# A transformer trunk's FFN: sixteen of twenty-two feature tiles of the second product by Strassen's scheme

## The chip, the cores and the metric

The kernel runs on one core of a Trainium2 chip. A core has TensorE (PE) for matrix products, which reads SBUF and writes PSUM; VectorE (DVE), ScalarE (ACT) and GpSimd (POOL) for elementwise work; and SyncE (SP), which here issues the DMAs. The metric is the device time of one execution in microseconds. Before the change the median of three runs is 2638.42 us (2637.98 to 2640.49).

## The reference, cut to what matters

Four layers work on x of 512 tokens by 1024 columns, in float32. Each has a token mixer (latent attention, retention, gated linear attention, and latent attention again) and then a dense FFN:

```
def swiglu_ffn(x, w_in, w_out):            # w_in 1024 x 5632, w_out 2816 x 1024
    gate, up = jnp.split(x @ w_in, 2, axis=-1)
    return (jax.nn.silu(gate) * up) @ w_out
x = layer_norm(DEEPNORM_ALPHA * x + mixer(x), ln_g[i, 0], ln_b[i, 0])
x = layer_norm(DEEPNORM_ALPHA * x + swiglu_ffn(x, ffn_w_in[i], ffn_w_out[i]), ln_g[i, 1], ln_b[i, 1])
```

## The kernel before

Every product is made of three matmuls (`mm3`, L126). Each float32 operand is split into a high part, a cast by ScalarE to the type that TensorE multiplies, and a low part, the rest, by a subtraction on VectorE (`split`, L101). The terms are high x high, high x low and low x high.

Weights come in chunks of 512 KB (`wcols`, `wload`): a DMA on SP's queue into one of three raw buffers `wraw`, and then `wsplit` (L116) into one of six pairs `whi`, `wlo`. For the first six chunks after a layer norm that ends a sub-layer (`relieve`), GpSimd makes the low part instead of VectorE, so that VectorE is free for the norm.

The FFN (`ffn`, L298) has 22 feature tiles of 128. For each tile the first product takes two weight chunks (gate and up), each 8 x 3 matmuls with the weights stationary and all 512 tokens moving. `evac` then takes silu(gate) on ScalarE and the product with up on VectorE, and splits the result h into a pair of tiles. The first three tiles go in two halves of 256 tokens, since the last tokens of x are not yet transposed.

The second product (`out_proj`, L213) follows when all 22 tiles are there: h is stationary by token tiles of 128, w_out moves by halves of 512 columns. For half 0, four PSUM tiles, one for each token tile, gather all 22 features, and `acc` (L178) adds them to alpha x x. For half 1, `out_tail` (L240) does the same until the last eight features; it keeps their four weight chunks and finishes one token tile after the other, 24 matmuls each, with the layer norm (`ln_finish`, L188) behind each. The transposes for the next mixer (`flush`, L165) are set two token tiles later. For few features (`nf <= 4`) `out_proj` instead loads all weight chunks first and goes by token tiles with both halves. Only mixers took that path.

PSUM has eight banks: six tiles of tag `ps` and two of tag `tp` for transposes. SBUF working tiles come from one pool in each phase (`phase`, L78), by tags with a number of buffers.

The order of instructions on each engine is fixed before the run: a scheduler takes the instructions in the order of the program as their priority, with times that it assumes for each, and hands out buffers as they come free by those times. At run time each engine follows its list in order and waits on semaphores.

Of the kernel before, what the change touches and what calls it, by code (L numbers as in the profile page):

```python
# [9 lines left out]
F32 = mybir.dt.float32  # L10
F32R = mybir.dt.float32r
I32 = mybir.dt.int32
AF = mybir.ActivationFunctionType
ALU = mybir.AluOpType
AX = mybir.AxisListType

P = 128
# [5 lines left out]
ALPHA = (2.0 * DEPTH) ** 0.25  # L23
# [3 lines left out]
NF = F // P  # L27
# [23 lines left out]
class Trunk:  # L51
# [25 lines left out]
    @contextmanager  # L77
    def phase(self, **tags):  # L78

        with self.tc.tile_pool(name="phase", bufs=1, reuse_waits="tile") as self.bp:  # L80
            self.tags = dict(tags, b=self.nb - sum(tags.values()))
            yield

    def b(self, shape=(P, 512), dt=F32, name="b", tag="b"):
# [127 lines left out]

    def out_proj(self, st, w, nf, coef, last, out=None, halves=(0, 1)):  # L213
        wf = lambda f0, half: self.wcols(w, f0 * P, 2, half * 512, 512)
        if nf <= 4:
            ch = {(c, hf): wf(2 * c, hf) for hf in halves for c in range(nf // 2)}
            for t in range(NT):
                for hf in halves:
                    ps = self.ps()
                    for f in range(nf):  # L220
                        if last and hf == 0 and f == 3:
                            self.flush(t - 2)
                        w2 = ch[f // 2, hf]
                        self.mm3(ps, st(f, t), (w2[0][:, f % 2, :], w2[1][:, f % 2, :]), f == 0, f == nf - 1)
                    self.acc(t, hf, ps, coef, last)
                if last:
                    self.ln_finish(t, out)
            self.relieve = 6 if last else 0
            return
        pss = [self.ps() for _ in range(NT)]  # L230
        for f in range(nf):
            if f % 2 == 0:
                w2 = wf(f, 0)
            for t in range(NT):
                self.mm3(pss[t], st(f, t), (w2[0][:, f % 2, :], w2[1][:, f % 2, :]), f == 0, f == nf - 1)
        for t in range(NT):
            self.acc(t, 0, pss[t], coef, last)
        self.out_tail(st, lambda f0: wf(f0, 1), nf, coef, last, out)
# [56 lines left out]
            self.proj_tile(t, wk, n, evac)  # L295


    def ffn(self, l, out=None):  # L298
        nc = self.nc
        w_in, w_out = self.ins["ffn_w_in"][l], self.ins["ffn_w_out"][l]  # L300
        hs = []

        def evac(pg, pu):
            s = self.b()
            nc.scalar.activation(s, pg, AF.Silu)
            nc.vector.tensor_tensor(s, pu, s, op=ALU.mult)  # L306
            h = self.bpair()
            self.split(h[0], h[1], s)
            hs.append(h)

        nh = 3
        first = []
        for f in range(nh):
            wg = self.wcols(w_in, 0, KT, f * P, P)
            wu = self.wcols(w_in, 0, KT, F + f * P, P)
            first.append((wg, self.ps()))
            first.append((wu, self.ps()))
        for t0 in (0, 2):
            for n, (w2, ps) in enumerate(first):
                self.proj_f(w2, ps[:, t0 * P : (t0 + 2) * P], KT, lambda k: self.xm(k, t0, t0 + 2))  # L320
                if n % 2:
                    self.flush(2 + n // 2)
        for f in range(nh):
            evac(first[2 * f][1], first[2 * f + 1][1])
        rot = False
        for f in range(nh, NF):
            if f == nh + 1:
                rot = self.before(l + 1, nc.vector)
            if f == NF - 4 and rot:
                self.rope_sin()  # L330
            wg = self.wcols(w_in, 0, KT, f * P, P)
            pg = self.ps()
            self.proj_f(wg, pg, KT, self.xm)
            wu = self.wcols(w_in, 0, KT, F + f * P, P)
            pu = self.ps()
            self.proj_f(wu, pu, KT, self.xm)
            evac(pg, pu)
        self.ln_begin(l, 1)
        st = lambda f, t: (hs[f][0][:, t * P : (t + 1) * P], hs[f][1][:, t * P : (t + 1) * P])
        self.out_proj(st, w_out, NF, ALPHA, True, out)  # L340

    def load_x(self, x):

# [805 lines left out]
    def run(self, out):  # L1149
        self.load_x(self.ins["x"][0])  # L1150
        for i in range(DEPTH):
            self.mixer(i)
            with self.phase():
                self.ffn(i, out[0] if i == DEPTH - 1 else None)


# [38 lines left out]
```

## Time and profile before

| what | value |
|---|---|
| median of three runs | 2638.42 us |
| the profiled execution | 2635.14 us |
| its span, first to last instruction | 2633.3 us |
| mean granted TensorE clock | 0.994 |
| TensorE busy | 2578.4 us (98%) |
| VectorE busy | 1416.0 us (54%) |
| ScalarE busy | 905.5 us (34%) |
| GpSimd busy | 220.6 us (8%) |
| DMA, mean over the span | 88 GB/s |

The rows further down come from one profiled execution. "L103" is a line of the kernel. A row of the timeline has the start, the duration, the engine, the line, the operation and its tiles (out<-in), and in brackets the idle time of that engine just before it with what ended it. The four FFNs lie at about 250 to 607, 1056 to 1410, 1675 to 2028 and 2270 to 2622 us.

### The profile page before, as it was taken

What the parts mean: (1) busy time and instruction counts of PE and PEld (TensorE: products, weight loads), DVE (VectorE), ACT (ScalarE), POOL (GpSimd) and SP (SyncE); (2) the same over time, 40 slices, a digit from 0 to 9 for tenths busy, and PEclk for the clock granted to TensorE, in tenths of its full rate; (3) what the DMA queues carried; (4) which work ended last, traced back from release to release, by engine and by line L of the source; (5) the groups of instructions that cost most, each with busy time, mean ns of one, the idle gap of its engine ahead of it and who ended that gap; (6) DMA issues with size and microseconds to landing.
All of it is one profiled execution on the core that took longest, in us unless ns stands there. A gap on an engine that the chain in (4) does not pass through costs nothing.

```text
span 2633.3 us, 32309 instructions
## 1 busy us (share of the span) xinstructions
PE 2578.4 (98%) x12996; PEld 2191.5 (83%) x12996; DVE 1416.0 (54%) x2484; ACT 905.5 (34%) x1381; POOL 220.6 (8%) x231
## 2 busy tenths in 40 slices
PE   7999999999999999999999999999999999999998
PEld 6888888887888888988888998888888788888886
DVE  6877433228755548333326888833335686633334
ACT  4652323213333332322213654322312564322221
POOL 3002000001110103000002011100002200100001
PEclk9999999999999999999999999999999999999999
DMA  4212433233223232333233212333322221333321
GB/s 144 73 41 68 128 96 96 96 96 88 77 76 95 89 92 83 103 98 97 96 95 95 76 61 65 109 96 96 96 96 77 70 74 46 100 96 97 99 93 56
DMA packets 294711, 232.35 MB, mean 88 GB/s; under 512 B 21120, under 2 KB 244480, under 8 KB 294560
## 3 DMA queue, kind: packets, MB, share of 16 engines
q1 hardware_dynamic: 294560, 230.28, 28.8%
q8 instruction: 102, 1.67, 0.3%
q14 instruction: 49, 0.40, 0.0%
HBM read 228.15 MB, written 2.10 MB: 87 GB/s over the span
## 4 chain that ended last, share of the span: by engine, by line
PE 85%; DVE 9%; POOL 2%; issue 2%; ACT 2%; DMA 1%; DVEq 0%; SPq 0%; ACTq 0%; POOLq 0%
PE ps L128 27%; PE ps L130 27%; PE ps L129 27%; DVE xt L205 2%; DVE xt L206 1%; PE tp L557 1%; DVE lnst L186 1%; DVE xl L103 1%; PE ps L538 1%; DVE lnu L145 1%; PE ps L537 1%; DMA wraw<-in_mla_w_down 0%; DVE xt L184 0%; PE tp L158 0%; DVE bl L103 0%
## 5 line engine op out<-in xcount | busy, mean ns | idle before, releaser
L102 ACT CAST whi<-wraw 128x1024 fp32r<-128x1024 f32 (+3 forms) x414 | 431.0, 1042 | 1122.3 <-PE ps L130 379.4
L103 DVE TENSOR_TENSOR wlo<-wraw,whi 128x1024 fp32r<-128x1024 f32 (+2 forms) x366 | 444.1, 1215 | 660.4 <-ACT whi L102 647.8
L129 PE MATMUL ps<-xl,whi 128*128 128x512 f32 (+1 forms) x1792 | 659.9, 368 | 7.9 <-DVE xl L103 7.9
L128 PE MATMUL ps<-xh,whi 128*128 128x512 f32 (+1 forms) x1792 | 660.3, 368 | 0.0
L130 PE MATMUL ps<-xh,wlo 128*128 128x512 f32 (+1 forms) x1792 | 659.4, 368 | 0.0
L129 PEld LDWEIGHTS ps<-xl,whi 128*128 128x128 f32 x1792 | 341.2, 190 | 63.1 <-DVE xl L103 8.7
L128 PEld LDWEIGHTS ps<-xh,whi 128*128 128x128 f32 x1792 | 341.2, 190 | 54.9 <-issue 0.4
L130 PEld LDWEIGHTS ps<-xh,wlo 128*128 128x128 f32 x1792 | 341.0, 190 | 55.1
L128 PE MATMUL ps<-whi,bh 128*128 128x512 f32 (+1 forms) x960 | 368.7, 384 | 0.2 <-ACT bh L102 0.2
L130 PE MATMUL ps<-whi,bl 128*128 128x512 f32 (+1 forms) x960 | 367.2, 383 | 0.0
L129 PE MATMUL ps<-wlo,bh 128*128 128x512 f32 (+1 forms) x960 | 367.0, 382 | 0.0
L130 PE MATMUL ps<-whi,xl 128*128 128x512 f32 (+3 forms) x752 | 262.9, 350 | 5.2 <-DVE xl L103 5.2
L128 PE MATMUL ps<-whi,xh 128*128 128x512 f32 (+3 forms) x752 | 264.9, 352 | 1.1 <-ACT xh L102 1.1
L129 PE MATMUL ps<-wlo,xh 128*128 128x512 f32 (+3 forms) x752 | 262.1, 349 | 0.1
L103 POOL TENSOR_TENSOR wlo<-wraw,whi 128x1024 fp32r<-128x1024 f32 (+4 forms) x48 | 118.8, 2490 | 1649.1 <-ACT whi L102 1637.0
L130 PEld LDWEIGHTS ps<-whi,bl 128*128 128x128 f32 x960 | 180.5, 188 | 35.5 <-DVE bl L103 0.5
L128 PEld LDWEIGHTS ps<-whi,bh 128*128 128x128 f32 x960 | 180.5, 188 | 35.0 <-ACT bh L102 0.8
L129 PEld LDWEIGHTS ps<-wlo,bh 128*128 128x128 f32 x960 | 180.5, 188 | 34.7
L306 DVE TENSOR_TENSOR b<-ps,b 128x512 f32<-128x512 f32 x88 | 60.8, 691 | 262.1 <-PE ps L130 261.4
L130 PEld LDWEIGHTS ps<-whi,xl 128*128 128x128 f32 x752 | 142.8, 190 | 23.3 <-DVE xl L103 6.4
L128 PEld LDWEIGHTS ps<-whi,xh 128*128 128x128 f32 x752 | 143.2, 190 | 18.7 <-ACT xh L102 1.5
L129 PEld LDWEIGHTS ps<-wlo,xh 128*128 128x128 f32 x752 | 143.0, 190 | 17.3 <-POOL wlo L103 0.5
(220 smaller groups left out, 2772.6 us busy)
## 6 DMA issues: line engine op xcount, KB each, us to landing
wraw<-in_ffn_w_in SPq DMA_DIRECT2D x176, 512.0 KB, 3.8
wraw<-in_ffn_w_out SPq DMA_DIRECT2D x88, 512.0 KB, 3.3
wraw<-in_ret_w_in SPq DMA_DIRECT2D x48, 512.0 KB, 3.8
wraw<-in_gla_w_in SPq DMA_DIRECT2D x22, 512.0 KB, 3.5
wraw<-in_mla_w_o SPq DMA_DIRECT2D x16, 512.0 KB, 3.9
wraw<-in_ret_w_o SPq DMA_DIRECT2D x16, 512.0 KB, 4.7
wraw<-in_mla_w_down SPq DMA_DIRECT2D x8, 512.0 KB, 4.4
wraw<-in_mla_w_ukv SPq DMA_DIRECT2D x8, 512.0 KB, 3.7
```

The source lines that it names most:

```text
L102: a = self.nc.scalar.copy(hi, src)
L103: b = (eng or self.nc.vector).tensor_tensor(lo, src, hi.bitcast(F32), op=ALU.subtract)
L128: mm(out, s[0], m[0], start=start, stop=False)
L129: mm(out, s[0], m[1], start=False, stop=False)
L130: mm(out, s[1], m[0], start=False, stop=stop)
L145: stt(u, y, y, x, op0=ALU.mult, op1=ALU.mult)
L186: nc.vector.bn_stats(self.stats[t][:, half * 6 : half * 6 + 6], x)
L205: nc.vector.scalar_tensor_tensor(x[:, sl], x[:, sl], mv[:, 0:1], self.g[:, sl], op0=ALU.subtract, op1=ALU.mult)
L206: nc.vector.scalar_tensor_tensor(x[:, sl], x[:, sl], r, self.bb[:, sl], op0=ALU.mult, op1=ALU.add)
L306: nc.vector.tensor_tensor(s, pu, s, op=ALU.mult)
L537: nc.tensor.matmul(ps, qr[:, sl], krh, start=False, stop=False)
L538: nc.tensor.matmul(ps, qr[:, sl], krz[e], start=False, stop=True)
```

## The change

For the first 16 feature tiles the second product becomes a 2 x 2 block product. The blocks of h are (tokens 0 to 255, 256 to 511) x (even, odd feature tile of a pair), those of w_out (even, odd tile) x (columns 0 to 511, 512 to 1023). Seven products of blocks, in Winograd's form, take the place of eight.

- `evac` writes the four h blocks of a pair of tiles into one tile `ft`, and GpSimd makes three sums and differences more (four instructions, with one in place). The seven factors of 128 x 256 are split together (`fh`, `fl`, 1792 elements for each partition).
- `ffn_out` (new) handles a chunk of two pairs, that is four feature tiles. It loads the four weight blocks, makes their sums in place on VectorE (four subtractions), splits each factor (seven splits instead of four), multiplies (for each product two token tiles x two pairs x three matmuls), and adds each result to one or two blocks of x in SBUF, or to a shared sum `u` that is added to three blocks at the end.
- A chunk starts after the first product of the tile behind its last one (tiles 4, 8, 12, 16). Its seven products are dealt out two, two, two and one behind the next four tiles; the last chunk's over the last six.
- The last six tiles go the plain way, now by the path by token tiles (`nf <= 6`): six weight chunks are loaded first, and each token tile takes 36 matmuls.
- The FFN's phase has its own numbers of buffers: 8 of `fh`, 1 of `ft`, 3 of `t` for weight blocks, 1 of `u`, 10 of `b`.

```diff
--- before.py
+++ after.py
@@ -78,7 +78,7 @@
     def phase(self, **tags):
 
         with self.tc.tile_pool(name="phase", bufs=1, reuse_waits="tile") as self.bp:
-            self.tags = dict(tags, b=self.nb - sum(tags.values()))
+            self.tags = {"b": self.nb - sum(tags.values()), **tags}
             yield
 
     def b(self, shape=(P, 512), dt=F32, name="b", tag="b"):
@@ -212,7 +212,7 @@
 
     def out_proj(self, st, w, nf, coef, last, out=None, halves=(0, 1)):
         wf = lambda f0, half: self.wcols(w, f0 * P, 2, half * 512, 512)
-        if nf <= 4:
+        if nf <= 6:
             ch = {(c, hf): wf(2 * c, hf) for hf in halves for c in range(nf // 2)}
             for t in range(NT):
                 for hf in halves:
@@ -295,18 +295,44 @@
             self.proj_tile(t, wk, n, evac)
 
 
     def ffn(self, l, out=None):
         nc = self.nc
         w_in, w_out = self.ins["ffn_w_in"][l], self.ins["ffn_w_out"][l]
-        hs = []
-        def evac(pg, pu):
+        ns = 16
+        self.fact, hs = {}, {}
+        self.u = self.b((P, 2, 512), tag="u", name="u")
+        half = lambda a: a.rearrange("p (a n) -> p a n", a=2)
+        def evac(f, pg, pu):
             s = self.b()
             nc.scalar.activation(s, pg, AF.Silu)
-            nc.vector.tensor_tensor(s, pu, s, op=ALU.mult)
-            h = self.bpair()
-            self.split(h[0], h[1], s)
-            hs.append(h)
+            if f >= ns:
+                if f < NF - 2:
+                    if f % 2 == 0:
+                        self.hp = self.b((P, 2, 512), F32R, "hh", "fh"), self.b((P, 2, 512), F32R, "hl", "fh")
+                    h = tuple(x[:, f % 2, :] for x in self.hp)
+                else:
+                    h = self.bpair()
+                nc.vector.tensor_tensor(s, pu, s, op=ALU.mult)
+                self.split(h[0], h[1], s)
+                hs[f] = h
+                return
+            if f % 2 == 0:
+                self.ft = self.b((P, 7, 256), tag="ft", name="ft")
+            ft = self.ft
+            nc.vector.tensor_tensor(ft[:, 2:4, :] if f % 2 else ft[:, 1::-1, :], half(pu), half(s), op=ALU.mult)
+            if f % 2:
+                tt = nc.gpsimd.tensor_tensor
+                tt(ft[:, 4, :], ft[:, 0, :], ft[:, 3, :], op=ALU.add)
+                tt(ft[:, 5, :], ft[:, 4, :], ft[:, 1, :], op=ALU.subtract)
+                tt(ft[:, 0, :], ft[:, 1, :], ft[:, 0, :], op=ALU.subtract)
+                tt(ft[:, 6, :], ft[:, 2, :], ft[:, 5, :], op=ALU.subtract)
+                h = self.b((P, 7, 256), F32R, "fh", "fh"), self.b((P, 7, 256), F32R, "fl", "fh")
+                self.split(h[0], h[1], ft)
+                self.fact[f // 2] = h
 
         nh = 3
         first = []
@@ -321,8 +347,9 @@
                 if n % 2:
                     self.flush(2 + n // 2)
         for f in range(nh):
-            evac(first[2 * f][1], first[2 * f + 1][1])
+            evac(f, first[2 * f][1], first[2 * f + 1][1])
         rot = False
+        todo = []
         for f in range(nh, NF):
             if f == nh + 1:
                 rot = self.before(l + 1, nc.vector)
@@ -334,10 +361,84 @@
             wu = self.wcols(w_in, 0, KT, F + f * P, P)
             pu = self.ps()
             self.proj_f(wu, pu, KT, self.xm)
-            evac(pg, pu)
+            evac(f, pg, pu)
+            if 4 <= f < ns + 4 and f % 4 == 0:
+                c = f // 4 - 1
+                todo = self.ffn_out(w_out, 2 * c, 2, c == 0)
+            left = (4 - f % 4) if f < ns else NF - f
+            for _ in range(-(-len(todo) // left) if todo else 0):
+                todo.pop(0)()
+        for tt in range(2):
+            for hf, c in ((0, 1), (1, 0), (1, 1)):
+                x = self.xt[2 * hf + tt][:, c * 512 : c * 512 + 512]
+                nc.vector.tensor_tensor(x, x, self.u[:, tt, :], op=ALU.add)
         self.ln_begin(l, 1)
-        st = lambda f, t: (hs[f][0][:, t * P : (t + 1) * P], hs[f][1][:, t * P : (t + 1) * P])
-        self.out_proj(st, w_out, NF, ALPHA, True, out)
+        st = lambda f, t: tuple(x[:, t * P : (t + 1) * P] for x in hs[ns + f])
+        self.out_proj(st, w_out[ns * P :], NF - ns, None, True, out)
+    def ffn_out(self, w, g0, n, begin):
+        nc = self.nc
+        rows = w[2 * g0 * P : 2 * (g0 + n) * P, :].rearrange("(g a p) c -> a p g c", a=2, p=P)
+        B = {}
+        def load(name, a, c, t):
+            nc.sync.dma_start(t, rows[a][:, :, c * 512 : c * 512 + 512])
+            B[name] = t
+        wt = lambda: self.b((P, n, 512), name="wt", tag="t")
+        sub = lambda to, x, y: nc.vector.tensor_tensor(B[to], B[x], B[y], op=ALU.subtract)
+        def product(name, slot, to, u=None):
+            hi, lo = self.wsplit(B[name], n, 512)
+            ps = [self.ps() for _ in range(2)]
+            for tt in range(2):
+                for i in range(n):
+                    s2 = tuple(x[:, slot, tt * P : (tt + 1) * P] for x in self.fact[g0 + i])
+                    self.mm3(ps[tt], s2, (hi[:, i, :], lo[:, i, :]), i == 0, i == n - 1)
+                for hf, c, first in to:
+                    self.acc(2 * hf + tt, c, ps[tt], ALPHA if first else None, False)
+                if u is not None:
+                    x = self.u[:, tt, :]
+                    if u:
+                        nc.scalar.copy(x, ps[tt])
+                    else:
+                        nc.vector.tensor_tensor(x, ps[tt], x, op=ALU.add)
+        s3, a11, a12, a22, s1, s2, s4 = range(7)
+        def p1():
+            load("1", 0, 0, self.wp.tile([P, n, 512], F32, tag="wraw", name="wraw", bufs=self.nraw))
+            load("2", 0, 1, wt())
+            load("3", 1, 1, wt())
+            product("1", a11, [(0, 0, begin)], begin)
+        def p5():
+            sub("1", "2", "1")
+            product("1", s1, [(0, 1, begin), (1, 1, begin)])
+        def p6():
+            sub("1", "3", "1")
+            load("4", 1, 0, wt())
+            product("1", s2, [], False)
+        def p2():
+            product("4", a12, [(0, 0, False)])
+        def p3():
+            sub("4", "4", "1")
+            sub("2", "3", "2")
+            product("3", s4, [(0, 1, False)])
+        def p7():
+            product("2", s3, [(1, 0, begin), (1, 1, False)])
+        def p4():
+            product("4", a22, [(1, 0, False)])
+        return [p1, p5, p6, p2, p3, p7, p4]
 
     def load_x(self, x):
 
@@ -1150,7 +1251,7 @@
         self.load_x(self.ins["x"][0])
         for i in range(DEPTH):
             self.mixer(i)
-            with self.phase():
+            with self.phase(fh=8, ft=1, t=3, u=1, b=10):
                 self.ffn(i, out[0] if i == DEPTH - 1 else None)
```

## Rows read from the trace of the kernel before

**Rows 1.** The page's busy times, with share of the span and instructions of each engine

```profile
PE 2578.4 (98%) x12996; PEld 2191.5 (83%) x12996; DVE 1416.0 (54%) x2484; ACT 905.5 (34%) x1381; POOL 220.6 (8%) x231
```

**Rows 2.** Busy us of each engine in stretches, with granted clock, DMA share and GB/s

```profile
262.00:592.00 330.00, 330.00 (x1524) 276.30 (x1524) 116.20 (x135) 90.52 (x109) 4.79 (x2) 1.00 0.34 102
...
2280.00:2617.00 337.00, 337.00 (x1552) 281.87 (x1551) 116.03 (x140) 88.10 (x106) 2.60 (x2) 1.00 0.30 91
```

**Rows 3.** Timeline of TensorE, first product: start us, us, instruction

```profile
359.69 0.39 PE L129 MATMUL ps<-xl,whi 128*128 128x512 f32 x1
...
371.93 0.39 PE L129 MATMUL ps<-xl,whi 128*128 128x512 f32 x1
```

**Rows 4.** Timeline of ScalarE and VectorE there; in brackets idle time before, and releaser

```profile
360.84 1.05 ACT L102 CAST whi<-wraw 128x1024 fp32r<-128x1024 f32 x1 [3.84 <-PE ps L129]
...
361.93 1.23 DVE L103 TENSOR_TENSOR wlo<-wraw,whi 128x1024 fp32r<-128x1024 f32 x1 [3.62 <-ACT whi L102]
...
366.54 0.69 DVE L306 TENSOR_TENSOR b<-ps,b 128x512 f32<-128x512 f32 x1 [3.38 <-PE ps L130]
```

**Rows 5.** Groups by form: line, engine, operation, shapes, count, busy us, mean ns of one

```profile
L103 DVE TENSOR_TENSOR wlo<-wraw,whi 128x1024 fp32r<-128x1024 f32 x355 | 435.6, 1228 | 652.5 <-ACT whi L102 640.1
...
L102 ACT CAST whi<-wraw 128x1024 fp32r<-128x1024 f32 x397 | 418.3, 1054 | 1104.4 <-issue 371.8 <-PE ps L130 370.1 <-PE ps L129 314.2
...
L103 POOL TENSOR_TENSOR wlo<-wraw,whi 128x1024 fp32r<-128x1024 f32 x42 | 106.4, 2549 | 1272.1 <-ACT whi L102 1260.1 <-DVE xt L184 9.0 <-issue 3.0
...
L103 DVE TENSOR_TENSOR bl<-b,bh 128x512 fp32r<-128x512 f32 x148 | 101.3, 685 | 12.3 <-ACT bh L102 12.0
...
L102 ACT CAST bh<-b 128x512 fp32r<-128x512 f32 x148 | 91.8, 621 | 57.6 <-DVE b L679 20.8 <-DVE b L753 19.0 <-DVE b L1024 11.1
...
L184 DVE SCALAR_TENSOR_TENSOR xt<-xt,ps 128x512 f32<-128x512 f32 x64 | 43.0, 682 | 77.3 <-PE ps L130 77.2
...
L792 POOL TENSOR_TENSOR b<-b 128x512 f32<-128x512 f32 x16 | 22.0, 1377 | 338.8 <-DVE gny L149 246.5 <-DVE b L791 82.7 <-DVE gny L147 8.1
```

**Rows 6.** DMA issues: buffer<-tensor, queue, operation, count, KB each, median us to landing

```profile
wraw<-in_ffn_w_in SPq DMA_DIRECT2D x176, 512.0 KB, 3.8
wraw<-in_ffn_w_out SPq DMA_DIRECT2D x88, 512.0 KB, 3.3
```

**Rows 7.** Timeline of GpSimd at the first FFN's end

```profile
579.81 2.40 POOL L103 TENSOR_TENSOR wlo<-wraw,whi 128x1024 fp32r<-128x1024 f32 x1 [334.43 <-ACT whi L102]
...
585.25 2.40 POOL L103 TENSOR_TENSOR wlo<-wraw,whi 128x1024 fp32r<-128x1024 f32 x1 [3.04 <-ACT whi L102]
...
603.82 10.22 POOL L103 TENSOR_TENSOR wlo<-wraw,whi 128x1024 fp32r<-128x1024 f32 x4 [16.17 <-ACT whi L102]
```

**Rows 8.** Timeline of VectorE at the first FFN's end

```profile
603.51 0.74 DVE L205 SCALAR_TENSOR_TENSOR xt<-xt,lnmv,ln_g 128x512 f32<-128x512 f32 x1
...
604.24 2.84 DVE L205 SCALAR_TENSOR_TENSOR xt<-xt,lnmv,ln_g 128x512 f32<-128x512 f32 x1
...
609.27 0.68 DVE L103 TENSOR_TENSOR xl<-tp,xh 128x512 fp32r<-128x512 f32 x1
```

**Rows 9.** Timeline of TensorE at the start of the second mixer

```profile
623.57 0.80 PE L130 MATMUL ps<-whi,xl 128*128 128x512 f32 x1 [3.75 <-DVE xl L103]
...
625.01 0.63 PE L130 MATMUL ps<-whi,xl 128*128 128x512 f32 x1
625.44 0.63 PE L128 MATMUL ps<-whi,xh 128*128 128x512 f32 x1
```

**Rows 10.** Timeline of TensorE and VectorE at the kernel's end

```profile
2622.17 0.39 PE L130 MATMUL ps<-whi,bl 128*128 128x512 f32 x1
...
2622.60 0.69 DVE L184 SCALAR_TENSOR_TENSOR xt<-xt,ps 128x512 f32<-128x512 f32 x1
...
2624.42 0.96 DVE L205 SCALAR_TENSOR_TENSOR xt<-xt,lnmv,ln_g 128x512 f32<-128x512 f32 x1
...
2625.37 1.68 DVE L205 SCALAR_TENSOR_TENSOR xt<-xt,lnmv,ln_g 128x512 f32<-128x512 f32 x1
```

## The prediction

> **What bounds the kernel now.** I read the page's busy shares first: TensorE works 98% of the span, VectorE 54%, ScalarE 34%, GpSimd 8% [rows 1]. Busy shares mix stages, so next the stretches. In the FFN of a layer TensorE is busy in every microsecond, at granted clock 1.00 (the 2.4 GHz level); VectorE is busy about 35% of it, ScalarE 27%, GpSimd under 2%. The first and the last layer stand there; the two between read alike [rows 2]. So in the FFN the time is the number of matmuls by their pitch. The pitch comes from the starts, not from the 0.39 us of one record, since records overlap: 54 starts lie between 359.69 and 371.93 us, that is 0.2267 us each [rows 3]. What would have to break for another engine to count is the lead of the weights: ScalarE's cast of a weight chunk waits for TensorE to give back one of six hi/lo pairs, and VectorE then stands idle over 3 us, twice for each feature tile [rows 4].
>
> **Matmuls.** The second product of 16 feature tiles takes 16 tiles x 4 token tiles x 2 column halves x 3 terms = 384 matmuls of 512 columns. By the scheme it is 4 chunks x 7 products x 2 token tiles x 2 pairs x 3 terms = 336. So 48 go in each layer, 192 in all, and the other six tiles keep their 144. The new ones have the same form (128x128 stationary, 512 moving), so the same pitch: 192 x 0.2267 = 43.5 us. Since TensorE has no idle time there, all of it comes off the span, unless something new makes it wait.
>
> A sentence on a rule against this: the Trainium skill (TensorE: Matmul & The Clock Gate, "Back-to-back issue gap") gives 131 ns as the sustained spacing of 512-column matmuls in a real kernel. By that, the removed ones would give only 192 x 0.131 = 25 us. The trace disagrees: 0.2267 us over 54 in a row.
>
> **VectorE.** Durations by shape are in [rows 5]. For one chunk of four tiles: 7 weight splits instead of 4, at 1.23 us; 4 weight subtractions of the same shape at 1.23 (bounds 1.23 and, if it ran as two pieces of 512, 2 x 0.69); 16 additions of a product into x at 0.68; 4 into the shared sum u at 0.68. That is 8.6 + 4.9 + 10.9 + 2.7 = 27.1 us against 4.9 before. The factor tile has 1792 elements where two h tiles had 512 each: from 0.685 us at 512 and 1.228 at 1024 its low part comes to 2.04 us against 1.37. Over a layer: 4 x 22.2 + 8 x 0.67 + 6 last additions of u x 0.69, less 1.4 us of u that goes to ScalarE, is 97 us. In the densest four tiles of the first product TensorE has 4 x 48 + 84 = 276 matmuls, 62.6 us. VectorE has 8 x 1.23 + 4 multiplies x 0.69 [rows 4] + 2 x 2.04 + 27.1 = 43.8 us: 70%, not a bound. In layers 0 and 2 the rotary tables of the next layer fall into the first chunk and press it more.
>
> **ScalarE** gets 3 more casts a chunk at 1.05 us and 8 longer casts a layer (1.70 us by the same line through 621 and 1054 ns, against 1.24), with two copies 18 us a layer beside 90. It stays far from a bound.
>
> **GpSimd** makes the four factor sums of a pair, of 128x256. No row has that shape: 0.64 us (a quarter of 2.55 for 128x1024) and 1.38 us (what 128x512 takes) bound it; I take 0.79, on the line through these two rows. That is 25 us a layer.
>
> **DMA.** Each chunk loads four 512 KB pieces, as four tiles did. But three of them now go to tiles of their own, and the first keeps one of three raw buffers from the first product to the fifth, so first-product loads run two deep instead of three, for two loads in 11 to 16 us. Loads land in under 4 us [rows 6]; the six hi/lo pairs, used at 15 per 62.6 us, still give about 25 us of lead. The SP queue gets chunk loads between the others; a load that waits for its tile holds up those behind it, which the lead covers. I cost this at nothing; without the lead a landing of 4 us would show in full.
>
> **New waits, by the nearest margin.** A chunk's first product needs the factors of the tile pair just made. After the pair's last matmul: multiply 0.69, four GpSimd sums 3.2 (2.6 to 5.5), cast 1.70, low part 2.04, together 7.6 us (7.0 to 9.9). The cover is the next tile's 48 matmuls, 10.9 us, and the first five matmuls of the product, 1.1: 12.0 us, and 2.7 more in all but a layer's first chunk, whose predecessor's last product lies between. Spare: 4.4 us, or 7.1. Queueing eats from it: VectorE takes its instructions in order and is 70% taken. Behind a late factor step there stand weight splits (25 us of lead) and additions that free PSUM buffers (six, of which two products and one tile use six; a buffer is wanted again after some 10 us). I take 1 us a layer, 4 us (0 to 20).
>
> **The port that GpSimd and VectorE share.** At the end of the first FFN, four weight splits on GpSimd run back to back, 10.22 us for four where one alone takes 2.40 [rows 7]. Meanwhile VectorE's instructions with two SBUF operands wait for the ends of these: one takes 2.84 us, where the same form just before took 0.74; one with PSUM as a source passes at 0.68 [rows 8]. So VectorE loses, GpSimd hardly does: 0.16 us an instruction. For the factor sums: at most 8 x 0.79 = 6 us a chunk on VectorE, which brings it to 80%.
>
> **The hand-over to the next mixer.** Before, two of six hi/lo pairs were free, so the next mixer's first two splits ran 22 to 28 us before the FFN's end at 607.4, and four at it [rows 7]. After, the tail's six chunks hold all six pairs until the last token tile, so six splits of 2.55 us crowd about its end, and each lets about one two-operand instruction of VectorE's layer norm through. Against that, a token tile of the tail lasts 36 matmuls, 8.2 us, instead of 24, 5.4, so each norm starts 2.7 us sooner before the end. At the first hand-over TensorE already waits 3.75 us for VectorE, and its next matmuls run slow, 0.43 us apart [rows 9]. Two more splits are 5.1 us of blocked VectorE, less 2.7: +2.4 there; the two other hand-overs show smaller waits, I take +1 each: +4 in all (-8 to +15).
>
> **The end.** The last matmul starts at 2622.17 and the last token tile's addition at 2622.60, right behind it; but in the norm that follows, an instruction of 0.74 us takes 1.68, beside GpSimd's part of the norm before [rows 10]. With 8.2 us for each token tile GpSimd is done with that part sooner, and that one and its neighbour (0.96) are back at 0.74: -1.2 us.
>
> **Sum.** The profiled execution took 2635.14 us, span 2633.3 and 1.8 around it; the median of three runs is 2638.42, 3.3 more. -43.5 + 4 + 4 - 1.2 = -36.7, so 2598.4 profiled and 2601.7 as a median.
>
> **Rivals.**
> *Half the gain goes to small waits.* Products wait for subtracted weights, buffers or factors, 1 to 2 us for each of 16 chunks, since the engines' order is written down ahead of the run and VectorE is full at places. For it: 80% with the port; against it: 25 us of lead. At 1.3 us a chunk, 21 us in place of the 4: 2619.
> *Slower: the factor chain lies bare.* If each GpSimd sum waits out a VectorE split (4 x 1.23 = 4.9), both VectorE steps wait 2 us behind others and the cast 1.05, the 7.6 us become 17.6; TensorE then waits 5.6 us at a layer's first chunk and 2.9 at three more, 14.3 a layer, 57 in all in place of the 4: 2601.7 - 4 + 57 = 2655. It decides from 2.7 us a chunk (43.5 / 16). Against it: in the rows it is VectorE that waits. The Trainium skill (SBUF — State Buffer, "Who interferes with whom") says that whichever starts first holds the shared ports for the whole instruction; by that rule GpSimd can lose as VectorE does, and the 4.9 us would be real. The trace shows the one side only.
> *The hand-overs cost 8 us each*, with weights late and the clock down after each wait: 24 us instead of 4: 2622.
> *The rule of 131 ns.* If a removed matmul frees less than its pitch, because others close up already, 25 us come off: 2638.4 - 25 + 6.8 = 2620. Against it is the even pitch.
>
> **Chances.** Forecast 0.63, its own range 2590 to 2615 (the lower end: hand-overs better by 8, no waits among the products); half the gain 0.17; bare chain 0.12; hand-overs 0.06; the rule 0.02. The range 2590 to 2632 leaves out the bare chain and the worst of the half gains, and little below. Within 0.2% (5.3 us, about what measurement can tell from no change) I put 0.05, of the worst half gains and the mildest bare chains; slower 0.11; faster 0.84.
>
> **What would show it.** Right: 192 fewer matmuls at the same pitch; FFN stretches still without TensorE idle time, each some 10 us shorter; VectorE near 1800 us busy, GpSimd near 320; the first wait after the FFN near 6 us. Wrong: TensorE idle at the first product of chunks, released by the factor tile's low part or its cast (bare chain) or by a weight's low part (half gain); over 10 us of waits behind each FFN (hand-over). The forecast fails if idle time within the FFNs passes 20 us.

## The result, and the profile after

The changed kernel takes 2599.7 us (median of four runs, 2595.45 to 2601.17) against 2638.2 for the kernel before (also of four): a ratio of 0.9852, with a 95% interval of 0.9835 to 0.9869. Forecast were 2601.7 us and a range of 2590 to 2632. The profiled execution took 2595.45 us, its span 2593.7; that is 39.6 us under the span of before.

The page's busy times after, which answer to [rows 1]:

```profile
PE 2536.9 (98%) x12804; PEld 2156.5 (83%) x12804; DVE 1792.7 (69%) x2900; ACT 974.6 (38%) x1405; POOL 335.7 (13%) x359
```

There are 192 matmuls fewer, 12804 for 12996. VectorE has 377 us more and GpSimd 115 us. Two stretches of the FFNs after, to be held against [rows 2] (TensorE's busy time comes first behind the length, then weight loads, VectorE, ScalarE, GpSimd, granted clock, DMA share, GB/s):

```profile
262.00:592.00 330.00, 330.00 (x1533) 276.35 (x1532) 220.54 (x269) 109.69 (x119) 30.96 (x33) 1.00 0.31 94
...
2270.00:2580.00 310.00, 310.00 (x1369) 256.69 (x1368) 202.79 (x245) 98.21 (x106) 31.32 (x32) 1.00 0.29 89
```

TensorE still has no idle time there, and the two FFNs between read the same. VectorE went from 35% to 67%. The pitch of the new matmuls, from the first and the last of 24 in two products, to be held against [rows 3]:

```profile
300.81 0.39 PE L128 MATMUL ps<-whi,fh 128*128 128x512 f32 x1
...
306.02 0.39 PE L130 MATMUL ps<-whi,fl 128*128 128x512 f32 x1
```

From the first start to the last there are 23 pitches in 5.21 us, 0.2265 us each (0.2267 before). From its first silu to its last matmul the second FFN takes 330.45 us for 341.33 before; the difference of 10.88 us is 48 x 0.2267. The other three give 10.86 to 10.88.

Where the 39.6 us came from, by stages of the two traces:

| stage | forecast | measured |
|---|---|---|
| matmuls of the four FFNs | -43.5 | -43.5 |
| waits inside the FFNs | +4 | 0 |
| three hand-overs to a mixer | +4 | +6.1 |
| the end, from the last matmul | -1.2 | -2.1 |
| the start, to the first silu | 0 | -0.2 |
| span | -36.7 | -39.6 |

The hand-overs are read from the stretches between the last matmul of one FFN and the first silu of the next. They hold a whole mixer each, which the change does not touch, and the first matmuls of the next FFN. Before:

```profile
607.20:1068.30 461.10, 453.65 (x2115) 378.85 (x2114) 292.91 (x559) 148.65 (x189) 67.32 (x43) 0.99 0.29 87
1409.60:1686.60 277.00, 266.69 (x1807) 244.33 (x1806) 233.36 (x538) 140.91 (x272) 41.03 (x24) 0.99 0.26 77
2027.90:2284.10 256.20, 246.74 (x1420) 214.53 (x1419) 185.70 (x356) 121.14 (x234) 44.03 (x75) 0.99 0.24 71
```

and after:

```profile
596.20:1059.10 462.90, 453.54 (x2115) 378.27 (x2114) 294.77 (x559) 150.44 (x190) 69.28 (x44) 0.99 0.30 91
1389.60:1669.40 279.80, 268.29 (x1808) 245.51 (x1806) 234.06 (x538) 142.45 (x275) 42.17 (x25) 0.99 0.27 82
1999.90:2257.40 257.50, 246.45 (x1419) 214.65 (x1418) 186.70 (x360) 121.62 (x233) 39.84 (x74) 0.99 0.26 76
```

By these rounded bounds the stretches sum to 994.3 and 1000.2 us. Length less TensorE's busy time is its idle time: 27.2 us before, 31.9 after, so 4.7 of some 6 us are waits. Another 1.2 us stand in the busy time of the same matmuls (967.1 and 968.3). There the granted clock differs, which falls behind waits, as here after the first FFN:

```profile
608.00:614.00 6.00, 1.42 (x7) 0.84 (x5) 5.76 (x16) 0.59 (x1) 1.80 (x2) 1.00 0.11 43
614.00:620.00 6.00, 5.67 (x23) 4.64 (x24) 1.47 (x3) 0.48 (x2) 0.00 (x0) 0.72 0.01 3
```

TensorE works 1.42 of the first 6 us; in the next 6 the granted clock is 0.72 on average, so a part of them went at the lower of the two levels (1.2 GHz). TensorE's busy time times what the granted clock lacks of 1.00, added up over pieces of 4 us of the three stretches, gives an estimate of what the lower clock costs: 8.6 us before and 10.0 after.

The first hand-over after, in rows of GpSimd, VectorE and TensorE, to be held against [rows 7 to 9]:

```profile
590.05 9.94 POOL L103 TENSOR_TENSOR wlo<-wraw,whi 128x1024 fp32r<-128x1024 f32 x4 [110.31 <-ACT whi L102]
590.07 2.92 DVE L205 SCALAR_TENSOR_TENSOR xt<-xt,lnmv,ln_g 128x512 f32<-128x512 f32 x1
...
600.98 5.15 DVE L206 SCALAR_TENSOR_TENSOR xt<-xt,lny,ln_b 128x512 f32<-128x512 f32 x2
...
614.33 0.80 PE L130 MATMUL ps<-whi,xl 128*128 128x512 f32 x1 [4.91 <-DVE xl L103]
```

Here the FFN's last matmul starts at 596.15. GpSimd's splits begin 6 us before it, where two of six were done over 20 us before it in the old kernel, and go on (a fifth at 600.37, a sixth at 602.93) until 605.6. VectorE's norm of the third token tile waits through all of it: its last two instructions take 5.15 us, where the same pair of the token tile before, at 584.17, took 1.41. TensorE waits 4.91 us, for 3.75 before.

The end, to be held against [rows 10]:

```profile
2584.64 0.39 PE L130 MATMUL ps<-whi,bl 128*128 128x512 f32 x1
...
2585.07 0.69 DVE L182 TENSOR_TENSOR xt<-ps,xt 128x512 f32<-128x512 f32 x1 [2.25 <-PE ps L130]
...
2587.62 0.74 DVE L205 SCALAR_TENSOR_TENSOR xt<-xt,lnmv,ln_g 128x512 f32<-128x512 f32 x1
```

VectorE now stands idle 2.25 us before the last addition, and the norm's instruction that took 1.68 us takes 0.74.

### The profile page after: what moved, and what is told of

Its sections match the earlier page's. It is cut to its first block, busy times and chain, and to the rows that moved or that the text cites. A ratio compares the mean times of both kernels' runs of the same rounds, so it can differ in the third digit from the quotient of the medians.

```text
span 2593.7 us, 32609 instructions
## 1 busy us (share of the span) xinstructions
PE 2536.9 (98%) x12804; PEld 2156.5 (83%) x12804; DVE 1792.7 (69%) x2900; ACT 974.6 (38%) x1405; POOL 335.7 (13%) x359
## 4 chain that ended last, share of the span: by engine, by line
PE 85%; DVE 9%; ACT 2%; POOL 2%; issue 2%; DMA 1%; DVEq 0%; SPq 0%; ACTq 0%; POOLq 0%
PE ps L128 27%; PE ps L130 27%; PE ps L129 27%; DVE xt L205 2%; DVE xt L206 1%; PE tp L658 1%; DVE lnst L186 1%; DVE lnu L145 1%; DVE xl L103 1%; PE tp L158 1%; DVE xt L182 1%; DVE bl L103 1%; PE ps L639 1%; PE ps L638 0%; DVE wlo L103 0%
## 5 line engine op out<-in xcount | busy, mean ns | idle before, releaser
L102 ACT CAST whi<-wraw 128x1024 fp32r<-128x1024 f32 (+3 forms) x398 | 412.2, 1040 | 700.3 <-issue 261.3
L103 DVE TENSOR_TENSOR wlo<-wraw,whi 128x1024 fp32r<-128x1024 f32 (+2 forms) x350 | 430.5, 1240 | 203.9 <-ACT whi L102 196.5
L182 DVE TENSOR_TENSOR xt<-ps,xt 128x512 f32<-128x512 f32 x288 | 187.2, 682 | 35.8 <-PE ps L130 35.8
L128 PE MATMUL ps<-whi,fh 128*128 128x512 f32 x448 | 174.3, 389 | 0.0
L129 PE MATMUL ps<-wlo,fh 128*128 128x512 f32 x448 | 174.3, 389 | 0.0
L130 PE MATMUL ps<-whi,fl 128*128 128x512 f32 x448 | 174.3, 389 | 0.0
L326 DVE TENSOR_TENSOR ft<-ps,b 128x512 f32<-128x512 f32 x64 | 44.2, 691 | 142.5 <-PE ps L130 78.1
L102 ACT CAST whi<-wt 128x1024 fp32r<-128x1024 f32 x64 | 67.5, 1054 | 191.0 <-PE ps L129 128.4
L329 POOL TENSOR_TENSOR ft<-ft 128x256 f32<-128x256 f32 x32 | 23.6, 737 | 821.8 <-DVE ft L326 821.8
```

The lines of the kernel that those rows point to most:

```text
L102: a = self.nc.scalar.copy(hi, src)
L103: b = (eng or self.nc.vector).tensor_tensor(lo, src, hi.bitcast(F32), op=ALU.subtract)
L128: mm(out, s[0], m[0], start=start, stop=False)
L129: mm(out, s[0], m[1], start=False, stop=False)
L130: mm(out, s[1], m[0], start=False, stop=stop)
L182: nc.vector.tensor_tensor(x, ps, x, op=ALU.add)
```

## The experiments

Spans are those of the profiled executions; ratios are of medians to the kernel before in the same job, with 95% intervals. "As changed" is the kernel after.

**Twelve tiles by the scheme, ten by the old path and tail.**

```
-        ns = 16
+        ns = 12
...
-            left = (4 - f % 4) if f < ns else NF - f
+            left = 4 - f % 4
```

> Strassen's scheme for 12 feature tiles instead of 16; the other ten by the plain path with the tail of the kernel before (token tiles of 24 matmuls, four chunks held). Theory (the gain is the number of matmuls by their pitch, everything else of the products is hidden; the 6 us lost behind the FFNs come from the new tail): 36 x 4 = 144 matmuls fewer than before, 32.6 us, and the hand-overs and the end as before, so a span near 2600.7 us, with no TensorE idle time inside the FFNs and 3.75 us again as the longest wait behind the first. Rival (the products themselves bring the later waits, by the fuller VectorE): 4 us more, span 2605. Rival (a removed matmul gives 131 ns): 19 us off, span 2614.

2607.78 us, ratio 0.9884 (0.9868 to 0.9901), span 2607.8. The FFN stretches are 8.16 us shorter than before each (333.17 for 341.33 in the second), which is 36 x 0.2267, and TensorE never idles in them. So the gain goes by the count of matmuls. The waits right behind the FFNs are back too (the longest 3.8 us). Still the span is 7 us over the theory, and past the first rival's 2605. The three mixer stretches tell where:

```profile
599.10:1063.30 464.20, 455.48 (x2116) 379.46 (x2115) 293.08 (x559) 148.90 (x190) 67.32 (x43) 0.99 0.30 90
1396.50:1676.30 279.80, 269.47 (x1808) 246.91 (x1807) 233.48 (x538) 141.43 (x273) 40.92 (x24) 0.98 0.27 81
2009.50:2267.60 258.10, 248.04 (x1419) 215.41 (x1418) 185.96 (x356) 121.02 (x233) 43.66 (x75) 0.98 0.25 76
```

They sum to 1002.1 us, 7.8 more than before. Idle time is 29.1 us, 1.9 more; busy time is 973.0 us, 5.9 more, for the same count of matmuls, and the granted clock is 0.98 where it was 0.99. The estimate of what the lower clock costs is 14.9 us, 6.3 more than before, so the clock accounts for the busy time; why it fell more here is not shown. The idle time does not bear out the rival's 4 us of later waits. In one profile the clock's share can thus hide an effect of 6 us in the mixers. The medians move less: 29.5 us against the 32.6 of the count.

**The last six tiles by the path of before.**

```
-        if nf <= 6:
+        if nf <= 4:
...
-        nl = 8
+        nl = min(nf, 8)
```

> As changed, but the last six feature tiles go by the path of before: half 0 in four PSUM tiles first, then half 1 by token tiles of 18 matmuls, with three weight chunks held instead of six. Same number of matmuls. Theory (the later waits behind the FFNs come from six hi/lo pairs held to the last token tile, so that six weight splits of GpSimd crowd about the FFN's end): the next mixer's first three splits run early again, the waits behind the FFNs shrink by about the 6 us, span 2588 to 2591. Rival (what counts is VectorE's lag in the norms): token tiles last 4.1 us where VectorE needs 5.6 us for each, so it falls 4 to 6 us further behind at each of four ends, span 2605 to 2615.

2600.63 us, ratio 0.9859 (0.9845 to 0.9874), span 2598.0: between the two forecasts, and neither is right alone. With three chunks held, the three mixer stretches come to 991.9 us, 8.3 less than as changed and less than the 994.3 of before. But the FFNs are no longer without idle time; they are 7.8 us longer in all than as changed, most of it in the first:

```profile
267.40:601.60 334.20, 330.03 (x1508) 275.14 (x1508) 219.13 (x262) 110.69 (x121) 41.38 (x37) 1.00 0.33 100
```

Its 4.2 us of idle time stand before transposes at 597.55 and 600.30, behind VectorE's work on the norms: the lag of the second forecast. FFN and mixer together are 789.5 us for 792.0 as changed; the second pair gains 0.5, the third loses 2.3. The lag shows at the end too:

```profile
2584.30 0.39 PE L130 MATMUL ps<-whi,bl 128*128 128x512 f32 x1
...
2588.22 0.68 DVE L182 TENSOR_TENSOR xt<-ps,xt 128x512 f32<-128x512 f32 x1
```

TensorE's last matmul (first row) is over by 2584.7, but the last addition (second row) starts 3.5 us later, where as changed it follows at once; the end costs 4.6 us more than as changed. So the number of held chunks trades against the length of a token tile, and the net is nothing.

**Twenty tiles by the scheme, two plain.**

```
-        ns = 16
+        ns = 20
...
-                        if last and hf == 0 and f == 3:
+                        if last and hf == 0 and f == min(3, nf - 1):
```

> Strassen's scheme for 20 feature tiles; two remain, so that a token tile of the tail lasts 12 matmuls, 2.7 us, while VectorE needs some 7 us for each (two additions, two statistics, norm). Theory of counting alone: 48 matmuls fewer than as changed, 10.9 us, span 2583. Theory that the plain tail is what hides the norms: TensorE is through in 10.9 us while VectorE needs 28, so 10 to 17 us of waits appear behind each FFN and at the end, 30 to 50 us net of the gain, span 2613 to 2633; inside the FFNs still no idle time.

2619.68 us, ratio 0.9933 (0.9919 to 0.9948), span 2616.9: slower than as changed by 20 us in the medians and 23 in the spans, though 48 more matmuls are gone. The FFNs have no idle time; TensorE's longest wait of all (waited-for, total us, times, longest) is now

```profile
PE tp L158 <- DVE xt L206: 25.9, 8, 8.9
```

that is, the transposes wait for the norms' last step; as changed it was 8.6 us in five. The stretch behind the second FFN is 289.5 us for 279.8, and the end 10 us longer. The plain six tiles are what hides the norms.

**All seven products of a chunk together.**

```
-            left = (4 - f % 4) if f < ns else NF - f
+            left = 1
```

> As changed, but all seven products of a chunk stand together behind one tile of the first product instead of two, two, two and one behind four. Same work. Theory (25 us of lead of the weights and six PSUM tiles cover unevenness): VectorE has 27 us of work in 19 us of products, 8 us behind, which the lead covers; span within 3 us of 2594. Rival (the dealing out is needed): TensorE waits up to 8 us for each of 16 chunks, on a weight's low part or a PSUM buffer; span up to 2720, and VectorE or ScalarE as releaser of waits inside the FFNs.

2596.51 us, ratio 0.9846 (0.9831 to 0.9861), span 2593.8: no change, no idle time in the FFNs. Nothing hangs on dealing the products out evenly. That the lead of the weights and six PSUM tiles are what covers VectorE's lag (8 us by the estimate ahead of the run) fits this, but is not shown by it.

**The scheme undone, the dealing kept.** `evac` splits only the four h blocks; each weight block is split once and used in two plain products.

```
-        return [p1, p5, p6, p2, p3, p7, p4]
+        return pair("1", 0, 0, raw, (1, 0)) + pair("2", 0, 1, wt, (1, 0)) + pair("4", 1, 0, wt, (2, 3)) + pair("3", 1, 1, wt, (2, 3))
```

> The scheme undone, the dealing out kept: the four blocks of 16 feature tiles are multiplied plainly, eight products a chunk (four weight splits, no sums, no u), two behind each of four tiles; tail as changed. Theory (the gain is the 48 matmuls of a layer alone): the count is that of the kernel before, so FFN stretches of 340 to 341 us again, the hand-overs as changed (+5 us), the end 1 to 2 us shorter: within 6 us of before, 2636 to 2643. Rival (dealing the second product among the first is itself worth something, by fuller overlap): 2620 to 2632.

2637.55 us, ratio 1.0003 (0.9994 to 1.0013): as before the change. Its page:

```profile
PE 2582.5 (98%) x12996; PEld 2194.9 (83%) x12996; DVE 1583.2 (60%) x2708; ACT 903.0 (34%) x1349; POOL 220.3 (8%) x231
```

With all 12996 matmuls back the gain is gone. The FFN stretches are those of before to 0.01 us (341.33 in the second), without idle time, so the order of the work gave nothing there; the missing eighth of the products gave all. This kernel has the changed tail without the seven products, and its mixer stretches are

```profile
607.30:1071.10 463.80, 453.90 (x2116) 378.34 (x2115) 294.99 (x557) 150.62 (x191) 69.65 (x44) 0.99 0.30 91
1412.40:1691.40 279.00, 267.92 (x1808) 245.90 (x1807) 233.61 (x536) 142.72 (x275) 42.47 (x25) 0.99 0.27 83
2032.70:2291.70 259.00, 247.43 (x1419) 215.41 (x1418) 185.40 (x360) 121.94 (x234) 42.68 (x74) 0.98 0.25 76
```

with 32.6 us of idle time, where as changed there are 31.9 and before 27.2. So the later waits at the hand-overs come with the tail, and not from the products.

**VectorE splits the next mixer's weights behind the FFN.**

```
-            self.relieve = 6 if last else 0
+            self.relieve = 6 if last and nf <= 4 else 0
```

> As changed, but behind the FFN VectorE makes the low parts of the next mixer's first six weight chunks itself, not GpSimd. Theory (in the hand-over GpSimd's six splits of 2.5 us hold the port, and VectorE's norm waits): VectorE needs 6 x 1.23 = 7.4 us more of its own but is no longer blocked for up to 16 us; the waits behind the FFNs fall by 3 to 5 us each, span 2581 to 2588. Rival (VectorE is full there anyway, so that 7.4 us more delay the third token tile's norm as the block did): within 4 us of 2594 or up to 8 us longer.

2586.93 us, ratio 0.9809 (0.9794 to 0.9824), span 2586.3, as the theory had it. At the first hand-over VectorE's rows now read

```profile
593.15 0.74 DVE L205 SCALAR_TENSOR_TENSOR xt<-xt,lnmv,ln_g 128x512 f32<-128x512 f32 x1
593.81 0.22 DVE L145 SCALAR_TENSOR_TENSOR lnu<-lny,lnx 128x1 f32<-128x1 f32 x1
...
595.27 1.22 DVE L103 TENSOR_TENSOR wlo<-wraw,whi 128x1024 fp32r<-128x1024 f32 x1
...
597.21 1.22 DVE L103 TENSOR_TENSOR wlo<-wraw,whi 128x1024 fp32r<-128x1024 f32 x1
```

with the instruction that took 2.92 us at 0.74, and the splits in between at 1.22 for GpSimd's 2.40 to 2.64. TensorE's wait there falls from 4.91 us to 0.82. Most of the gain in the trace is in this first hand-over, 7.4 us; the other two give 2.4 and 0.4, and the first FFN begins 3.1 us later, for which I have no row. TensorE's wait, and the mixer stretch behind the first FFN:

```profile
612.71 0.50 PE L130 MATMUL ps<-whi,xl 128*128 128x512 f32 x1 [0.82 <-DVE xl L103]
...
599.20:1054.70 455.50, 450.86 (x2115) 376.46 (x2114) 289.80 (x556) 150.39 (x190) 61.21 (x40) 1.00 0.30 93
```

**VectorE makes the factor sums.**

```
-                tt = nc.gpsimd.tensor_tensor
+                tt = nc.vector.tensor_tensor
```

> As changed, but VectorE makes the four factor sums of a pair, not GpSimd (128 sums of 128x256, some 0.42 us each, 54 us of VectorE in all). Theory (VectorE has slack and the factor chain of 8.4 us has over 2 us of spare): TensorE's list is unchanged, no idle time inside the FFNs, span within 3 us of 2594. Rival (VectorE is near its bound in the dealt stretch): waits inside the FFNs of 1 us or more a chunk, 2610 or later.

2600.3 us, ratio 0.9861 (0.9846 to 0.9876), span 2596.9, with no idle time in the FFNs: no difference. GpSimd's part in the products was harmless, and not needed.

**Every product split made twice, then three times.**

```
             hi, lo = self.wsplit(B[name], n, 512)
+            nc.vector.tensor_tensor(lo, B[name], hi.bitcast(F32), op=ALU.subtract)
```

> As changed, but each of the 112 product splits makes its low part twice (VectorE, 1.23 us each, 138 us more). VectorE's share in the densest four tiles goes from 70% to 84%, over 90% with the port. Theory (it is a queue with 25 us of lead, and only its mean load counts): still no idle time of TensorE inside the FFNs, span within 4 us of 2594. Rival (waits begin well before 100%): 1 us or more for each chunk, 2610 to 2640, released by the low part of a weight or of a factor.

Twice: 2598.41 us, ratio 0.9852 (0.9835 to 0.9869), span 2596.2. No idle time in the FFNs, with VectorE busy for 50.8 us in a stretch of 62.6 us of a chunk, 81%.

> As changed, but each of the 112 product splits makes its low part three times (276 us more of VectorE). By the rows VectorE then has 43.8 + 17.2 = 61 us in the densest 62.6 us, and up to 6 us of waits at the port: 97 to 107%. Theory (VectorE's mean load is what would bound, and the change stands 30% below): now TensorE waits inside the FFNs, by a few us for each chunk, 10 to 70 us in all, span 2604 to 2664. Rival (the mean has room even here, or the lead absorbs it): within 4 us of 2594.

Three times: 2616.6 us, ratio 0.9917 (0.9903 to 0.9932), span 2616.4. Now TensorE waits inside the FFNs, and the first row of its waits names the place:

```profile
PE ps L130 <- DVE fl L103: 13.2, 16, 1.3
```

Sixteen waits, one for each chunk, all for the low part of the factors, at the sixth matmul of a chunk's first product, where the newer pair's low part is first used. The FFNs take 4.5 to 4.8 us longer each. A chunk's stretch in the first FFN:

```profile
362.60:425.20 62.60, 62.39 (x276) 51.36 (x275) 56.09 (x59) 20.55 (x21) 8.78 (x8) 1.00 0.31 93
```

VectorE is busy 90% of it, not the 97% that I had worked out, and still the chain is late. So the bare factor chain is the first thing to give, as the rival had it, but only with 276 us more on VectorE.

**No splits on GpSimd behind any norm.**

```
-            self.relieve = 6 if last else 0
+            self.relieve = 0
...
-        self.relieve = 6
+        self.relieve = 0
```

> As changed, but GpSimd makes no weight's low part behind any layer norm, neither at the FFN's end nor at a mixer's. Theory (the port is what costs, wherever the norms run): the FFN's starts gain too, 2 to 4 us each at four mixers' ends, span 2572 to 2580. Rival (at the mixers' ends a token tile lasts 24 matmuls or fewer, 5.4 us, and VectorE, which needs 5.6 to 7, has no room for six more splits): no gain or a loss there, span 2584 to 2596.

2561.97 us (2561.4 to 2562.69), ratio 0.9713 (0.9698 to 0.9727), span 2560.9: better than either theory had it, and the fastest of all kernels here, 38 us under the change and 76 under the kernel before. Its mixer stretches:

```profile
594.50:1045.30 450.80, 449.65 (x2115) 374.68 (x2114) 289.65 (x562) 150.58 (x190) 45.77 (x34) 1.00 0.31 94
1375.80:1642.70 266.90, 264.98 (x1807) 242.98 (x1806) 222.86 (x531) 142.47 (x274) 19.25 (x12) 1.00 0.29 87
1973.20:2224.60 251.40, 244.39 (x1419) 213.50 (x1419) 180.45 (x363) 121.74 (x234) 18.09 (x64) 0.99 0.26 79
```

The idle time falls from 31.9 us to 10.1; the busy time falls as well, 968.3 to 959.0 us at the same count of matmuls. The estimate of what the lower clock costs falls from 10.0 us to 1.6, which is most of these 9.3. So a wait is paid by its length and, where the clock falls behind it, by matmuls 0.43 us apart. The same edit was not run on the kernel before, so how much of the 38 us it would give there is not shown.

**The kernel before, without GpSimd's splits behind the FFN.**

```
-        self.relieve = 6
+        self.relieve = 0 if nf == NF else 6
```

> The kernel before, with VectorE instead of GpSimd for the next mixer's first six weight splits behind an FFN. Theory A (the blocked port cost before the change as well): 3 to 5 us at the first hand-over, less at the others, span 2626 to 2630. Theory B (it pays only with the changed tail, whose token tiles of 8.2 us leave VectorE room; before, at 5.4 us, GpSimd's help was worth its price): within 2 us of 2633 or longer.

2628.86 us, ratio 0.9968 (0.9955 to 0.998), span 2626.9: theory A. The help cost some 9 us before the change too; as changed its removal gives 12.8 (2599.7 to 2586.93), or some 11 by the two ratios, since the kernel before differed by 1.9 us between the two jobs. So the change did not bring this price. Whether it made it higher is not shown: the difference of some 3 us is within the intervals of the ratios. The mixer stretches of the profiled executions point that way, with some 10 us gained as changed and 6 before.

**Both: no splits on GpSimd behind the FFN, products together.** The two edits above in one.

> As changed, with no GpSimd splits behind the FFN and all seven products of a chunk together. Theory (the two edits touch different stretches, and bunching changed nothing): as the first alone, span within 4 us of 2586. Rival (the fuller VectorE needs the dealing when it is tighter): longer by more than 4 us.

2587.36 us, ratio 0.9809 (0.9794 to 0.9823), span 2585.5: the same as without the bunching.

## Why the prediction was right, step by step

**Matmuls times pitch.** This step carried the forecast and came out to the second digit: -43.5 us, 10.88 for each FFN. The first experiment shows it proportional (8.16 us for 36), and the plain eight products show it alone: all of them back, all of the gain gone. The rival by the 131 ns of the Trainium skill (TensorE: Matmul & The Clock Gate, "Back-to-back issue gap") would have given 6.3 us for each FFN (an estimate, 48 x 0.131); this case's runs show 0.2267 us for a removed matmul, and the measurement decides.

**VectorE's load.** Forecast +97 us for each layer, the page has 377 / 4 = 94. The stretch of a chunk, forecast at 43.8 of 62.6 us:

```profile
363.00:425.60 62.60, 62.60 (x278) 51.84 (x277) 42.44 (x45) 20.86 (x21) 7.47 (x8) 1.00 0.33 101
```

That is 68% for 70%. VectorE is no bound there, nor at 81%; at 90% the waits have begun. So the small waits that the first rival put at half the gain did not come.

**The factor chain.** Forecast 7.6 us, of which 3.2 on GpSimd. The trace shows this, one pair's chain on the three engines that take part, in order of time:

```profile
290.20 0.69 DVE L326 TENSOR_TENSOR ft<-ps,b 128x512 f32<-128x512 f32 x1 [1.47 <-PE ps L130]
290.97 0.74 POOL L329 TENSOR_TENSOR ft<-ft 128x256 f32<-128x256 f32 x1 [13.71 <-DVE ft L326]
291.03 1.76 DVE L103 TENSOR_TENSOR wlo<-wraw,whi 128x1024 fp32r<-128x1024 f32 x1
291.79 1.60 POOL L330 TENSOR_TENSOR ft<-ft 128x256 f32<-128x256 f32 x1
...
294.82 1.69 ACT L102 CAST fh<-ft 128x1792 fp32r<-128x1792 f32 x1 [3.82 <-POOL ft L332]
...
296.54 2.03 DVE L103 TENSOR_TENSOR fl<-ft,fh 128x1792 fp32r<-128x1792 f32 x1 [3.75 <-ACT fh L102]
```

From the multiply's start to the low part's end it is 8.37 us, and 8.36 to 8.38 in all but the first of 32 pairs. The parts were sized well: 0.74 for 0.79, 1.69 for 1.70, 2.03 for 2.04. What the forecast left to queueing was one hit at the port. VectorE's split at 291.03 waits for the first sum and takes 1.76 us instead of 1.23; the second sum then waits for that split and takes 1.60 instead of 0.74. Of a layer's first chunk, the product's first matmul starts 10.6 us after the multiply, and five more matmuls (1.1 us) stand before the first use of the low part; so 3.4 us of the 4.4 that I gave as spare were left, and the 4 us for waits were not needed. That GpSimd hardly loses was wrong in this place:

```profile
L330 POOL TENSOR_TENSOR ft<-ft 128x256 f32<-128x256 f32 x32 | 50.5, 1577 | 2.5
L331 POOL TENSOR_TENSOR ft<-ft 128x256 f32<-128x256 f32 x32 | 23.6, 737 | 0.0
```

Two groups by form (count, busy us, mean ns): the second sum loses 0.84 us on average over 32 pairs. The Trainium skill (SBUF — State Buffer, "Who interferes with whom") has it that whichever starts first holds the shared ports to its end; here the trace agrees, 1.577 us behind a split for 0.737 without. The bare chain needed four such hits and more queueing; one came.

**The hand-overs.** Forecast +4 us by two more splits crowded about the end; measured 4.7 us of waits and 1.2 of slower matmuls. The sum fits better than its parts: +2.4 was forecast for the first and +1 for each of the others, and the stretches give +1.9, +2.8 and +1.4; the longest wait behind the first FFN is 4.91 us, where the sign named was near 6. That GpSimd's splits cost time there is shown by their removal, some 11 to 13 us as changed; most of that was there before the change. That the increase comes with the tail is shown by the plain eight products, which have the tail and the same waits. That within the tail it is the six held chunks is only in part shown: with three held, the mixer stretches lost 8.3 us, but the shorter token tiles, which came with the same edit, cost 7.8 us in the FFNs. Why the third hand-over lost 2.3 us there stays open.

**The end.** -2.1 us for -1.2: the stretched instructions of the norm came back as forecast. The other 0.9 us lie behind VectorE's last instruction, and I have no row that explains them.

**The sum.** The spans fell by 39.6 us for a forecast of 36.7; 4 us too many for waits inside the FFNs and 2 too few at the hand-overs partly cancel. That the medians agree better (2599.7 for 2601.7) is luck: the profiled execution after was the fastest of its four.

## What to carry to other kernels

Where the trace shows one engine without a gap at an even pitch, a change is worth its removed instructions times the pitch, as long as the others stay clear of full; test that by loading them on purpose, not by their busy share. Look at what lies just outside the improved stretch: helpers that were placed to relieve an engine can block it, and here removing the help was worth nearly as much as the arithmetic. A tail of plain work that hides norms is worth keeping: removing 48 more matmuls made the kernel 20 us slower.

## What the runs showed of the hardware that was not expected

- GpSimd's splits next to VectorE's norms cost more than they save, behind the FFNs and behind the mixers taken together. A 128x1024 split is 2.40 to 2.64 us on GpSimd and 1.22 on VectorE, and beside it a VectorE instruction with two SBUF operands took 2.92 us for 0.74. Removing the help at all norms took 32.8 us off the span as changed (2593.7 to 2560.9).
- Two engines at this port take turns: an instruction of each waited once for the other (1.76 us for 1.23, then 1.60 for 0.74), so the loss is on both sides and depends on which starts first.
- After short waits in the mixers the matmuls run 0.43 us apart instead of 0.2267 for a while, at a granted clock of 0.72 over 6 us in the rows above. Over the three mixer stretches the busy time of the same matmuls (some 5340) was 959.0 us with 10.1 us of idle time, 968.3 with 31.9, and 973.0 with 29.1; by the estimate above the lower clock costs 1.6, 10.0 and 14.9 us of these. Each is one execution: the four of the changed kernel lie 5.7 us apart, at mean granted clocks of 0.990 to 0.994.
